# A two-layer hybrid decoder on one core: new order of the mixers' output projection and of the work around it, and seven low halves built by an adding transfer

## The chip, the cores and the metric

The kernel runs on one core of one Trainium2 chip. Its engines are TensorE (PE; its weight loads are listed as PEld), VectorE (DVE), ScalarE (ACT), GpSimd (POOL) and SyncE (SP), which issues nearly all transfers. The metric is the time of one execution on the device in microseconds, as the median of the runs.

## The reference

One sequence of 256 tokens with 1024 features passes through two layers. Each layer is FFN, mixer, FFN, and every part is wrapped in RMS norms:

```python
f = swiglu_ffn(rmsnorm(x, ffn1_norm_pre[i]), ffn1_w_in[i], ffn1_w_out[i])
x = x + 0.5 * rmsnorm(f, ffn1_norm_post[i])
h = rmsnorm(x, mix_norm_pre[i])
p = h @ mix_w_in[i]
qkv, z, beta_logit, a_logit, glu_in, gates = jnp.split(p, SPLITS, axis=-1)
y_a = gated_deltanet(qkv, z, beta_logit, a_logit, ...)
y_b = conformer_conv(glu_in, ...)
g_a, g_b = jnp.split(jax.nn.sigmoid(gates), 2, axis=-1)
y = (g_a * y_a + g_b * y_b) @ mix_w_out[i]
x = x + rmsnorm(y, mix_norm_post[i])
# and a second FFN as the first
```

`gated_deltanet` (8 heads of 128) runs a causal convolution of 4 taps and SiLU over q, k and v, normalizes q and k, solves a triangular system per chunk of 64 tokens, and scans over the chunks with a state per head; its output is normalized per head, `o = rmsnorm(o, norm_w) * silu(z)`, and multiplied by `gdn_w_o`. `conformer_conv` gates one half of its input by the sigmoid of the other, runs a causal convolution of 31 taps, a layer norm and SiLU, and multiplies by `cnv_w_o` and adds `b_o`. All is float32.

## The kernel before, in words

**Products in three parts.** Each float32 operand of a large product is split into a high half, rounded to the fast type, and a low half, the difference. A product is the sum of high by high, high by low and low by high, so each weight tile gives three PE instructions. The weights are cut into pieces of 128 x 1024 (512 KB). For every piece SP issues a transfer from memory to a tile `raw` (a ring of four), ACT rounds it to `whi` (`to_high`), and DVE or POOL subtracts: `wlo = raw - whi` (`to_low`); `whi` and `wlo` are rings of eight.

**The order of a mixer.** A mixer works off 17 chunks of columns of its input projection, in the order of the table `PLAN`: g0 to g3 (the convolution's input and its gates), k1, ka, kb (keys, and the logits of the decays), v, q, z, and a, b (the gates of the merger). Two further products with 1024 x 1024 weights follow, the heads' (`gdn_w_o`) and the convolution's (`cnv_w_o`), then the last with `mix_w_out`. In between run jobs of the other engines, each a generator that is moved on step by step: `f_*` takes a chunk's products out of the banks; `decays` and `dts` make the decays; `kt`, `qt`, `vt` the keys, queries and values (the short convolution's steps are `c`, its results `kT`, `qT`, `vT`); `sim` the similarities (`at`); `inv` the triangular inverse, on POOL (`iu`), whose result goes through memory (`dU`) into the tiles `u`; `merge` puts its blocks together on PE; `s0`, `s1` the scan (`vr`, `vn`, `o`); `c0` to `c3` the long convolution on DVE (`cacc`, `hT`); `cn`, `cn1` its norm (`bns`, `lnr`, `xhat`, transposed again and through SiLU into `cf` and `ct`); `on0`, `on` the norm of the heads (`vo`, `ro`, `ot`); `yt` the merged rows before the last product.

**What sets the order.** `PLAN` says at which chunk a job may start, `DELAY` how many groups of products lie between its steps, `AFTER` and `LATE` which jobs must be done before, and how long before. A planner counts time on the engines by simple costs (`vector_us`, `pool_us`) and gives each low half to DVE or POOL; DVE, POOL and ACT then work off their programs in exactly this order. `FILL` names the jobs that are used as filling, the long convolution on DVE and the inverse on POOL, in steps for which an engine has time (`ahead`, `aheadp`).

**The end of a mixer.** Before, the convolution's projection comes first: its eviction adds `b_o` and multiplies by the gate b. The heads' projection follows: its eviction multiplies by the gate a and adds the other. The normalization of q is not applied to q; the job `qs` computes `rq` and its square on POOL, and `o_scale` brings them into the norm of the heads.

Of the kernel before, what the change touches and what calls it, by code (L numbers as in the profile page):

```python
# [46 lines left out]
    "ffn": (3, 2, 8, 12, 0), "pre0": (12, 12, 10, 0, 21, 2), "pre1": (14, 43, 4, 12, 8), "yt0": (10, 0, 10, 10, 26),  # L47
    "yt1": (10, 2, 0, 3, 3), "f_g0": (3, 0, 2, 9, 1), "f_g1": (5, 1, 1, 1), "c0": (0, 16, 0),
    "f_k1": (0, 1, 3, 1, 1, 3), "f_ka": (3, 0, 3), "decays": (12, 4, 2, 15, 4), "dts": (50, 3, 0, 0, 19, 19),
# [15 lines left out]
    "qs": ("qt0", "qt1"), "s0": ("merge", "vt0", "vt1", "qt0", "qt1"), "s1": ("s0",),  # L65
    "cn": ("c0", "c1", "c2", "c3", "s1"), "cn1": ("cn",), "on": ("s1", "on0"), "on0": ("s0", "qs"),
# [6 lines left out]
LATE = {"inv": 20, "cn": 12, "sim0": 5, "sim1": 6, "merge": 7, "dts": 14}  # L73

POOL = {*range(7, 10), *range(11, 14), 16, *range(18, 21), 22, 23, 25, *range(29, 33), 35, 36, 38, 39, *range(41, 45), *range(47, 50), 51, 53, 55, 58, 60, 61, 63, *range(65, 69), *range(70, 73), 77, 78, 85}
# [11 lines left out]
CFG = dict(stat=1000, conv=50, ev=300, tok=4, st=4, post=-800, pre=1000, fin=None, turn=100, tokens=-100, glu=100, dec=200, dts=500, kt=300, vt=0, qt=50, inv=1000, sim=100, merge=-400, scan=50, norm=-800, onorm=-100, yt=-400, w=50, forms=100, far=14, depth=9, land=1.8, slack=1.2, apart=3, beat=1.0, tails=4, ahead=1.5, lag=6, free=3, aheadp=3, lag2=3, bias=2, held=1, urge=2.0, close=3.0)  # L87

KIND = {"f_g0": "glu", "f_g1": "glu", "f_g2": "glu", "f_g3": "glu", "decays": "dec", "dts": "dts", "kt0": "kt", "kt1": "kt",
        "vt0": "vt", "vt1": "vt", "qt0": "qt", "qt1": "qt", "qs": "qt", "inv": "inv", "sim0": "sim", "sim1": "sim",  # L90
# [237 lines left out]
class Stream:  # L328
# [51 lines left out]
    def load_one(self):  # L380
        i, p = self.nload, self.ringed()
        if self.planned:
            return
        c = slice(0, p.raw.src.shape[-1])
        if p.raw.tile is None:
            p.raw.tile = self.fresh()
            self.nc.sync.dma_start(p.raw.tile[:, c], p.raw.src)
        p.low = 0.0
        if self.lanes is not None:
            self.his.append((self.lanes.now + CFG["lag"], i, lambda: self.to_high(p, c)))  # L390
            self.lows.append((self.lanes.now + CFG["lag"] + CFG["lag2"], i, lambda eng: self.to_low(p, c, eng)))
# [12 lines left out]
    def tick(self, upto=-1):  # L404

        if self.planned:
            self.pump()
            return

        def due(job):  # L410
            return job[0] <= self.lanes.now or job[1] <= upto
        while self.his and due(self.his[0]):
            self.his.pop(0)[2]()
        while self.lows and due(self.lows[0]):
            job = self.lows.pop(0)
            first = self.gp.at + 2.4 <= self.vec.at + 1.2 + CFG["bias"] and job[1] < len(self.side) and self.gp.tc is not None
            job[2](self.gp if first else self.vec)

    def in_step(self, lanes):
        if lanes is None:  # L420
            self.tick(self.nload)
            self.lanes.stream = None
        else:
            lanes.stream = self
        self.lanes = lanes

    def plan(self, lanes):
        if lanes is not None:
            self.planned, self.lanes, lanes.stream, self.begun = True, lanes, self, self.pe.at
            self.raws = []  # L430
            for p in self.pieces[self.nload:self.nload + 120]:
                for raw in p.group:
                    if raw not in self.raws:
                        raw.first = p.n
                        self.raws.append(raw)
            self.out = []
        else:
            for p in self.pieces[self.taken:self.nload]:
                self.force(p)
            self.planned, self.lanes.stream, self.lanes = False, None, None  # L440

# [60 lines left out]
    def issue(self, eng, t, p, kind):  # L502
# [4 lines left out]
        for c in p.parts if p.form else [slice(0, n)]:  # L507
# [47 lines left out]
def trunk(ctx: ExitStack, tc: tile.TileContext, x_in, wfirst, consts, feat, pch, tokp,  # L555
# [103 lines left out]
    for l in range(depth):  # L659
# [10 lines left out]
        extend(m)  # L670
# [481 lines left out]
    def mixer(xt, l, after_mix):  # L1152
# [96 lines left out]
        rq = small(16, "rq", bufs=1)  # L1249
        rq2 = small(16, "rq2", bufs=1)  # L1250
# [257 lines left out]
        def q_tokens(gp):  # L1508
# [5 lines left out]
            V.tensor_scalar(vq[:, gp * 8:gp * 8 + 8], ss, float(P), P * 1e-6, op0=ALU.mult, op1=ALU.add)  # L1514
# [121 lines left out]
        def take(c):  # L1636
# [20 lines left out]
            "qs": lambda c: q_scale(), "cn": lambda c: conv_norm(), "cn1": lambda c: conv_out(1), "on": lambda c: o_norm(), "on0": lambda c: o_first(),  # L1657
# [76 lines left out]
        def o_scale(tb):  # L1734
# [5 lines left out]
            rqt, rq2t = (t.rearrange("p (g b h) -> p g b h", g=2, b=2)[:, :, tb, :] for t in (rq, rq2))  # L1740
# [36 lines left out]
        def ev_b(tb, acc):  # L1777
            for hf in range(2):
                cs = slice(hf * 512, hf * 512 + 512)
                yb = tokt("yb")  # L1780
                V.tensor_tensor(yb, acc[hf], bo[:, cs], op=ALU.add)
                gt = gate[f"b{hf}"][:, tb, :]
                V.scalar_tensor_tensor(gt, gt, 1.0, yb, op0=ALU.add, op1=ALU.mult)
# [3 lines left out]
        def ev_a(tb, acc):  # L1787
            yT[tb] = [slot(16 + 2 * hf + tb, [P, 2, 4, P], F32R, name="yt") for hf in range(2)]
            for hf in range(2):
                gt = gate[f"a{hf}"][:, tb, :]  # L1790
                V.scalar_tensor_tensor(gt, gt, 1.0, acc[hf], op0=ALU.add, op1=ALU.mult)
                V.tensor_tensor(gt, gt, gate[f"b{hf}"][:, tb, :], op=ALU.add)
# [134 lines left out]
```

## Time and profile before

| | |
|---|---|
| Runs | 1337.93, 1337.77, 1335.19 us |
| Median | 1337.77 us |
| The profiled execution, its own time | 1335.39 us |
| Its span, first to last instruction | 1333.2 us |
| Granted TensorE clock | 0.999 |
| PE busy | 1310.6 us, 98% of the span |
| DVE, ACT, POOL busy | 1031.1, 772.1, 369.4 us |
| Weights, one transfer from issue to landing (mixer) | 3.8 us |
| Moved in all | 273.78 MB |

The first layer's mixer lies at about 186 to 489 us of the span, the second's at about 847 to 1149. POOL works almost only in the mixers. The names to the left of an arrow are what an instruction writes, to the right what it reads; line numbers are often those of a helper through which all instructions of an engine pass (L134 for DVE and POOL, L154 and L160 for PE, L189 for ACT), so groups are told apart by names of tiles. Matmuls are pipelined, so PE's busy time counts an array that is fed without a break.

### The profile page before, as it was taken

The numbers are of one execution on the slowest core, as the hardware profiler recorded it, in microseconds if no ns is written. First come the engines' busy times: TensorE is split into PE (matmuls) and PEld (weight loads), VectorE is DVE, ScalarE is ACT, GpSimd is POOL, SyncE is SP. The second block draws the span as 40 slices with busy tenths as digits, with TensorE's granted clock in tenths as the row PEclk, the third lists the DMA queues.
The fourth block names the chain that finished last, engine by engine and source line by source line (L and its number), as shares of the span: only waits on it lengthen the run. The fifth ranks groups of instructions, "written<-read, shape, count | busy, mean of one in ns | idle before, by whom it ended". The sixth has DMA issues, their size and how long they took to land.

```text
span 1333.2 us, 20598 instructions
## 1 busy us (share of the span) xinstructions
PE 1310.6 (98%) x7376; PEld 1112.1 (83%) x7376; DVE 1031.1 (77%) x1812; ACT 772.1 (58%) x1263; POOL 369.4 (28%) x332
## 2 busy tenths in 40 slices
PE   9999999999999999999999999999999999999998
PEld 7887879997787888888888888799977878888886
DVE  6889655999975776897577895569999766678973
ACT  6566547676565545565455564577646664555751
POOL 0000017798853200000000000277998431000000
PEclk9999999999999999999999999999999999999999
DMA  8985846562643666858568768464536447587481
GB/s 300 305 268 157 297 158 206 175 209 100 191 149 137 229 231 211 263 176 275 189 234 271 239 193 273 138 234 165 186 119 200 157 135 246 176 279 243 155 295 50
DMA packets 115302, 273.78 MB, mean 205 GB/s; under 512 B 24160, under 2 KB 48256, under 8 KB 115200
## 3 DMA queue, kind: packets, MB, share of 16 engines
q1 hardware_dynamic: 114912, 272.40, 61.5%
q8 instruction: 58, 0.95, 0.3%
q14 instruction: 44, 0.36, 0.1%
q10 hardware_dynamic: 288, 0.07, 0.0%
HBM read 256.68 MB, written 15.75 MB: 204 GB/s over the span
## 4 chain that ended last, share of the span: by engine, by line
PE 74%; DVE 14%; ACT 4%; DMA 3%; issue 2%; POOL 1%; DVEq 0%; POOLq 0%; ACTq 0%; SPq 0%
PE mm L154 69%; DVE cacc L134 4%; DVE wlo L134 4%; PE gd L154 3%; DVE c L134 2%; DMA raw<-mw 2%; ACT whi L189 2%; PE tr L160 2%; DMA raw<-w1i 1%; DVE at L134 1%; ACT dt L189 1%; DVE sum L134 1%; ACT sg L189 0%; DMA raw<-w2i 0%; DVE qT L134 0%
## 5 line engine op out<-in xcount | busy, mean ns | idle before, releaser
L154 PE MATMUL mm<-whi,xt 128*128 128x512 f32 (+1 forms) x1888 | 598.7, 391 | 3.6 <-ACT qT L189 2.2
L189 ACT CAST whi<-raw 128x1024 fp32r<-128x1024 f32 (+1 forms) x424 | 435.0, 1035 | 282.7 <-PE mm L154 61.1
L134 DVE TENSOR_TENSOR wlo<-raw,whi 128x1024 fp32r<-128x1024 f32 (+1 forms) x316 | 377.0, 1211 | 110.3 <-ACT whi L189 107.6
L154 PEld LDWEIGHTS mm<-whi,xt 128*128 128x128 f32 x1888 | 352.5, 188 | 77.0 <-ACT qT L189 3.0
L154 PE MATMUL mm<-wlo,xt 128*128 128x512 f32 (+1 forms) x944 | 365.0, 387 | 0.0
L134 POOL TENSOR_TENSOR wlo<-raw,whi 128x1024 fp32r<-128x1024 f32 (+1 forms) x108 | 253.9, 2368 | 145.0 <-ACT whi L189 142.7
L154 PE MATMUL mm<-whi,act 128*128 128x512 f32 x704 | 218.5, 390 | 0.0
L154 PEld LDWEIGHTS mm<-wlo,xt 128*128 128x128 f32 x944 | 177.5, 188 | 34.0 <-DVE wlo L134 0.7
L134 POOL TENSOR_TENSOR rpost<-ss,exp 128x1 f32<-128x1 f32 x12 | 6.5, 539 | 661.8 <-DVE ss L134 661.8
L134 DVE SCALAR_TENSOR_TENSOR cacc<-hT,pc,cacc 128x254 f32<-128x254 f32 (+28 forms) x464 | 179.4, 467 | 0.2
L154 PE MATMUL mm<-xt,whi 128*128 128x256 f32 x960 | 175.5, 285 | 0.8 <-ACT qT L189 0.6
L154 PEld LDWEIGHTS mm<-whi,act 128*128 128x128 f32 x704 | 132.2, 188 | 27.8 <-DVE ag L134 0.5
L154 PEld LDWEIGHTS mm<-xt,whi 128*128 128x128 f32 x960 | 149.3, 192 | 1.9 <-ACT qT L189 0.9
L154 PE MATMUL mm<-wlo,act 128*128 128x512 f32 x352 | 137.2, 390 | 0.5 <-DVE wlo L134 0.5
L154 PE MATMUL mm<-xt,wlo 128*128 128x256 f32 x480 | 135.7, 283 | 0.0
L154 PEld LDWEIGHTS mm<-xt,wlo 128*128 128x128 f32 x480 | 91.9, 192 | 0.0
L154 PEld LDWEIGHTS mm<-wlo,act 128*128 128x128 f32 x352 | 66.1, 188 | 14.6 <-DVE wlo L134 1.2
L189 ACT ACTIVATE ag<-mm,rstd 128x256 f32<-128x256 f32 x80 | 35.4, 470 | 30.0 <-PE mm L154 28.5
L189 ACT ACTIVATE jk<-mm 128x512 f32<-128x512 f32 x24 | 14.4, 598 | 63.2 <-PE mm L154 63.2
L134 DVE TENSOR_TENSOR act<-way,act 128x512 fp32r<-128x512 f32 x44 | 30.3, 689 | 21.1 <-ACT act L189 21.1
L134 DVE SCALAR_TENSOR_TENSOR ag<-mm,rstd,ag 128x256 f32<-128x256 f32 x80 | 35.8, 479 | 13.5 <-ACT ag L189 13.5
L134 DVE SCALAR_TENSOR_TENSOR c<-mm,pc,c 128x255 f32<-128x255 f32 (+2 forms) x108 | 43.7, 476 | 2.3 <-ACT c L189 2.3
(217 smaller groups left out, 1457.6 us busy)
## 6 DMA issues: line engine op xcount, KB each, us to landing
raw<-mw SPq DMA_DIRECT2D x168, 512.0 KB, 3.8
raw<-w2i SPq DMA_DIRECT2D x80, 512.0 KB, 4.9
raw<-w1i SPq DMA_DIRECT2D x76, 512.0 KB, 4.9
raw<-w1o SPq DMA_DIRECT2D x44, 512.0 KB, 4.5
raw<-w2o SPq DMA_DIRECT2D x44, 512.0 KB, 4.7
way<-way SPq DMA_DIRECT2D x112, 64.0 KB, 2.3
way<-way SPq DMA_DIRECT2D x28, 256.0 KB, 4.0
wbc<-feat SPq DMA_DIRECT2D x13, 512.0 KB, 5.0
```

Source lines behind the costliest of these rows:

```text
L134: r = op(out, *a, **k)
L154: r = self.eng.matmul(o, w, x, **k)
L160: r = self.eng.transpose(*a)
L189: r = op(out, *a, **k)
```

## The change

Six things change, in both mixers alike; the order of the chunks and PE's number of products stay.

1. The heads' projection comes first, the convolution's second, with the pieces of their weights in that order too. The heads' eviction (`ev_o`) multiplies by gate a and adds gate b times `b_o`; the convolution's (`ev_c`) multiplies by gate b and adds. One more DVE operation for each half row.
2. The job `qs` is gone. The sum of q's squares is scaled with the norm's epsilon, and `o_scale` forms its denominator with one DVE operation where POOL had two, and no product by `rq` after the power.
3. `PLAN`, `DELAY` and `LATE` are new, which moves jobs against the chunks.
4. The planner's cost of a DVE operation, its lead on POOL and its bias between DVE and POOL are a little different.
5. `ADDS` names pieces by their number within a mixer, seven of which exist. For these ACT writes the negative of the high half into the low half's tile (a second instruction of 1024 columns), and POOL issues a transfer that fetches the weights from memory again and adds them there. No `raw - whi` is computed for them.
6. Where the tables of ACT's functions change, its program has 14 table loads in all, before 10.

Counted over the program: POOL's tensor operations 302 to 274 (16 of the 28 are low halves), its small scalar operations 8 to 4, its transfers 0 to 14; DVE 978 three-operand steps where 966 were and two more low halves; ACT 14 more activations.

```diff
+ADDS = set((3, 9, 27, 31, 32, 34, 47, 51, 54, 55, 58, 59, 61))
...
+            self.fed += 1
+            p.adds = self.fed in ADDS
...
             self.act.copy(p.hi[:, c], p.raw.part(c))
+            if p.adds:
+                self.act.activation(p.lo[:, c], p.hi.bitcast(F32)[:, c], AF.Copy, scale=-1.0)
+
+    def add_raw(self, p):
+        with prio(self.tc, "w"):
+            self.gp.dma_start(p.lo[:, :p.raw.src.shape[-1]], p.raw.src, accum_op=ALU.add)
...
             job = self.lows.pop(0)
+            if job[3].adds:
+                self.add_raw(job[3])
+                continue
...
-        extend(m)
+        m = list(m)
+        extend(m[8:16] + m[:8] + m[16:])
...
-            V.tensor_scalar(vq[:, gp * 8:gp * 8 + 8], ss, float(P), P * 1e-6, op0=ALU.mult, op1=ALU.add)
+            V.tensor_scalar(vq[:, gp * 8:gp * 8 + 8], ss, P * RMS_EPS, P * 1e-6 * RMS_EPS, op0=ALU.mult, op1=ALU.add)
...
-        def q_scale():
-            yield from ()
-            power(rq, vq, -0.5)
-            W.tensor_tensor(rq2, rq, rq, op=ALU.mult)
...
-            W.tensor_tensor(ve, rq2t, sso, op=ALU.mult)
-            W.tensor_scalar(v8, v8, 1.0 / P, RMS_EPS, op0=ALU.mult, op1=ALU.add)
+            V.scalar_tensor_tensor(ve, sso, 1.0 / P, vqt, op0=ALU.mult, op1=ALU.add)
             power(r8, v8, -0.5)
-            W.tensor_tensor(ro, ro, rqt, op=ALU.mult)
...
+        lanes.finish(last["on"])
+        proj_out(head_part, 8, ev_o)
         lanes.finish(last["cn"])
-        proj_out(lambda kt, tb: part(cT[tb], kt), 8, ev_b, need=lambda: last["cn1"])
-        lanes.flush()
-        proj_out(head_part, 8, ev_a)
+        proj_out(lambda kt, tb: part(cT[tb], kt), 8, ev_c, need=lambda: last["cn1"])
```

How the order moves is shown at three places of the first mixer. The first is PE around the convolution's norm: `hT` is the convolution's output, `xhat` its normalized rows, `ct` what the convolution's projection multiplies and `ot` what the heads' does. Before:

```order
L154 MATMUL mm<-wlo,xt 128x512
L154 MATMUL mm<-whi,xt 128x512
L160 MATMUL tr<-cst,hT_1787 128x128 x4
L160 MATMUL tr<-cst,hT_1788 128x128 x4
L160 MATMUL tr<-cst,xhat 128x128 x8
L154 MATMUL mm<-whi,ct 128x512
L154 MATMUL mm<-wlo,ct 128x512
```

and now:

```order
L179 MATMUL tr<-cst,hT_1787 128x128 x4
L179 MATMUL tr<-cst,hT_1788 128x128 x4
L173 MATMUL mm<-whi,ot 128x512
L173 MATMUL mm<-wlo,ot 128x512
L173 MATMUL mm<-whi,ot 128x512 x2
L173 MATMUL mm<-wlo,ot 128x512
L173 MATMUL mm<-whi,ot 128x512
L179 MATMUL tr<-cst,xhat 128x128 x4
L173 MATMUL mm<-whi,ot 128x512
```

The transposes of `xhat` stood right behind those of `hT` and right ahead of the products that read their result; they now stand among the products of the heads' projection, and four at a time.

The second is ACT at the decays, whose exponentials are `aexp` and `eo`; `kT` is the keys' SiLU and `sg` the sigmoid of the convolution's gates, read from the banks that PE fills next. Before:

```order
L189 ACT_TABLE_LOAD
L189 ACTIVATE aexp<-tp 128x16
L189 ACTIVATE eo<-ba 128x16
L189 CAST whi<-raw 128x1024
L189 ACTIVATE eo<-ein 128x16
L189 CAST whi<-raw 128x1024
L189 ACTIVATE sg<-mm,bgh 128x256
L189 ACTIVATE sg<-sg 128x256
L189 CAST whi<-raw 128x1024
L189 ACTIVATE sg<-mm,bgh 128x256
```

and now:

```order
L208 ACTIVATE eo<-ba 128x16
L208 CAST whi<-raw 128x1024
L208 ACT_TABLE_LOAD
L208 ACTIVATE kT_1790<-c_2136 128x256
L208 ACT_TABLE_LOAD
L208 ACTIVATE eo<-ein 128x16
L208 ACTIVATE sg<-mm,bgh 128x256
L208 CAST whi<-raw 128x1024
L208 ACTIVATE sg<-sg 128x256
L208 CAST whi<-raw 128x1024
L208 ACT_TABLE_LOAD
L208 ACTIVATE kT_1790<-c_2137 128x256
```

Two steps of `kT`, which stood ahead of this stretch, now lie within it, each behind a table load of its own, and another load leads back to the exponential.

The third is POOL at the end of the inverse (`iu`) in the first mixer. Before:

```order
L134 TENSOR_TENSOR iu<-iu 128x14x4
L134 TENSOR_TENSOR wlo<-raw,whi 128x1024
L134 TENSOR_TENSOR iu<-iu,ia 128x45
L134 TENSOR_TENSOR iu<-iu 128x15x3
L134 TENSOR_TENSOR iu<-iu,ia 128x30
L134 TENSOR_TENSOR iu<-iu 128x15x2
L134 TENSOR_TENSOR iu<-iu,ia 128x16
L134 TENSOR_TENSOR iu<-iu 128x16
L134 TENSOR_TENSOR wlo<-raw,whi 128x1024 x5
L134 TENSOR_TENSOR rq<-vq,exp_80 128x16
```

and now:

```order
L153 TENSOR_TENSOR iu<-iu,ia 128x70
L153 TENSOR_TENSOR iu<-iu 128x14x5
L153 DMA wlo<-mw 128x1024
L153 TENSOR_TENSOR iu<-iu,ia 128x56
L153 TENSOR_TENSOR iu<-iu 128x14x4
L153 TENSOR_TENSOR iu<-iu,ia 128x45
L153 TENSOR_TENSOR iu<-iu 128x15x3
```

The row `DMA wlo<-mw` is an adding transfer that POOL issues; four of them stand between steps of the inverse, and one low half that POOL computes. Before, two low halves stood there.

More of the change, by code (lines that the diff above doesn't have):

```diff
@@ L38 @@
 PLAN = [
[4 rows of a table removed]
+    ("g0", ["f"]),
+    ("k1", ["f", "sim1", "c1"]),
+    ("ka", ["f", "decays", "dts"]),
+    ("g1", ["f", "c0", "inv", "kt1"]),
+    ("kb", ["f", "kt0"]),
+    ("g3", ["f", "sim0"]),
+    ("g2", ["f"]),
+    ("v1", ["f", "vt1", "c3"]),
+    ("q0", ["f", "s1", "qt1", "c2", "vt0"]),
+    ("q1", ["f", "s0"]),
+    ("v0", ["f", "qt0"]),
+    ("z0", []),
+    ("z1", ["merge", "on0", "on"]),
+    ("a0", []),
+    ("b0", ["cn1"]),
+    ("b1", []),
+    ("a1", ["cn"]),
 ]
@@ L46 @@
     "first": (0,), "forms": (57, 0, 6, 0, 1), "begun": (1, 0), "later": (0, 0, 1, 1), "gate": (0, 1), "gates": (0, 1, 1),
[L47 to L49 removed]
[8 rows of a table removed]
+    "ffn": (3, 2, 8, 12, 0), "pre0": (10, 12, 18, 0, 21, 1), "pre1": (15, 35, 4, 4, 0), "yt0": (7, 1, 0, 27, 3),
+    "yt1": (2, 12, 0, 11, 4), "f_g0": (0, 8, 0, 3, 21), "f_g1": (0, 5, 2, 3), "c0": (24, 16, 11),
+    "f_k1": (4, 2, 13, 1, 0, 3), "f_ka": (4, 0, 8), "decays": (12, 4, 3, 15, 4), "dts": (0, 3, 0, 0, 32, 8),
[8 rows of a table added]
 }
@@ L64 @@
     "qt0": ("f_q0", "vt0"), "qt1": ("f_q1", "vt1"),
-    "qs": ("qt0", "qt1"), "s0": ("merge", "vt0", "vt1", "qt0", "qt1"), "s1": ("s0",),
-    "cn": ("c0", "c1", "c2", "c3", "s1"), "cn1": ("cn",), "on": ("s1", "on0"), "on0": ("s0", "qs"),
+    "s0": ("merge", "vt0", "vt1", "qt0", "qt1"), "s1": ("s0",),
+    "cn": ("c0", "c1", "c2", "c3", "s1"), "cn1": ("cn",), "on": ("s1", "on0"), "on0": ("s0", "qt0", "qt1"),
 }
@@ L71 @@
 FILL = (("c3", "c2", "c1", "c0"), ("inv",))
-LATE = {"inv": 20, "cn": 12, "sim0": 5, "sim1": 6, "merge": 7, "dts": 14}
-POOL = {*range(7, 10), *range(11, 14), 16, *range(18, 21), 22, 23, 25, *range(29, 33), 35, 36, 38, 39, *range(41, 45), *range(47, 50), 51, 53, 55, 58, 60, 61, 63, *range(65, 69), *range(70, 73), 77, 78, 85}
+LATE = {"inv": 23, "cn": 7, "sim0": 3, "sim1": 5, "merge": 0, "dts": 14, "qt1": 0, "kt0": 1, "vt1": 14, "s0": 3, "qt0": 0, "vt0": 20, "s1": 0, "kt1": 0}
+POOL = {9, 10, 12, 13, 22, 23, 25, 26, 27, 30, 31, 32, 35, 38, 41, 42, 44, 46, 47, 53, 54, 56, 58, 59, 63, 64, 65, 66, 67, 70, 72, 73, 78, 82, 85}
 UNITS = 4*((9,),)
@@ L85 @@
 USERS = {"12": (("t1", "summed"),), "22": (("22", "low"), ("t2", "summed")), "11": (("t3", "low"),), "21": (("21", "low"), ("t4", "summed"))}
-CFG = dict(stat=1000, conv=50, ev=300, tok=4, st=4, post=-800, pre=1000, fin=None, turn=100, tokens=-100, glu=100, dec=200, dts=500, kt=300, vt=0, qt=50, inv=1000, sim=100, merge=-400, scan=50, norm=-800, onorm=-100, yt=-400, w=50, forms=100, far=14, depth=9, land=1.8, slack=1.2, apart=3, beat=1.0, tails=4, ahead=1.5, lag=6, free=3, aheadp=3, lag2=3, bias=2, held=1, urge=2.0, close=3.0)
+ADDS = set((3, 9, 27, 31, 32, 34, 47, 51, 54, 55, 58, 59, 61))
+CFG = dict(stat=1000, conv=50, ev=300, tok=4, st=4, post=-800, pre=1000, fin=None, turn=100, tokens=-100, glu=100, dec=200, dts=500, kt=300, vt=0, qt=50, inv=1000, sim=100, merge=-400, scan=50, norm=-800, onorm=-100, yt=-400, w=50, forms=100, far=14, depth=9, land=1.8, slack=1.2, apart=3, beat=1.0, tails=4, ahead=1.5, lag=6, free=3, aheadp=3.5, lag2=3, bias=1.5, held=1, urge=2.0, close=3.0)
 KIND = {"f_g0": "glu", "f_g1": "glu", "f_g2": "glu", "f_g3": "glu", "decays": "dec", "dts": "dts", "kt0": "kt", "kt1": "kt",
-        "vt0": "vt", "vt1": "vt", "qt0": "qt", "qt1": "qt", "qs": "qt", "inv": "inv", "sim0": "sim", "sim1": "sim",
+        "vt0": "vt", "vt1": "vt", "qt0": "qt", "qt1": "qt", "inv": "inv", "sim0": "sim", "sim1": "sim",
         "merge": "merge", "s0": "scan", "s1": "scan", "cn": "norm", "cn1": "norm", "on": "onorm", "on0": "onorm",
@@ L104, in pool_us, with plain_us @@
     return 0.2 + (4e-3 if name == "tensor_scalar" else 1e-3) * size
+def plain_us(name, size, k):
+    return 0.1 + size / 960.00
 class Clocked:
@@ L301, in __init__ @@
         self.raw, self.form, self.use, self.n = raw, form, use, 0
+        self.adds = False
         self.hi = self.lo = self.summed = self.high = self.low = None
@@ L389, in load_one @@
         if self.lanes is not None:
+            self.fed += 1
+            p.adds = self.fed in ADDS
             self.his.append((self.lanes.now + CFG["lag"], i, lambda: self.to_high(p, c)))
-            self.lows.append((self.lanes.now + CFG["lag"] + CFG["lag2"], i, lambda eng: self.to_low(p, c, eng)))
+            self.lows.append((self.lanes.now + CFG["lag"] + CFG["lag2"], i, lambda eng: self.to_low(p, c, eng), p))
             return
@@ L423, in in_step @@
         else:
-            lanes.stream = self
+            lanes.stream, self.fed = self, 0
         self.lanes = lanes
@@ L515, in issue @@
                 self.to_low(p, c, eng)
+        if eng is self.vec:
+            k = len(p.parts if p.form else [0])
+            eng.at = t + k * 0.1 + n / 960.0
         setattr(p, {"sum": "summed"}.get(kind, kind), eng.at)
@@ L1774, in mixer, with ev_o @@
         bo = load_feat(l, R_BO, 4)
[L1777 to L1783, printed above, removed]
-        yT = [None, None]
-        def ev_a(tb, acc):
-            yT[tb] = [slot(16 + 2 * hf + tb, [P, 2, 4, P], F32R, name="yt") for hf in range(2)]
+        def ev_o(tb, acc):
             for hf in range(2):
@@ L1791, in ev_a, with ev_c @@
                 V.scalar_tensor_tensor(gt, gt, 1.0, acc[hf], op0=ALU.add, op1=ALU.mult)
-                V.tensor_tensor(gt, gt, gate[f"b{hf}"][:, tb, :], op=ALU.add)
+            for hf in range(2):
+                gt, yb = gate[f"a{hf}"][:, tb, :], tokt("yb")
+                V.scalar_tensor_tensor(yb, gate[f"b{hf}"][:, tb, :], 1.0, bo[:, hf * 512:hf * 512 + 512], op0=ALU.add, op1=ALU.mult)
+                V.tensor_tensor(gt, gt, yb, op=ALU.add)
+        yT = [None, None]
+        def ev_c(tb, acc):
+            yT[tb] = [slot(16 + 2 * hf + tb, [P, 2, 4, P], F32R, name="yt") for hf in range(2)]
+            for hf in range(2):
+                gt, gb = gate[f"a{hf}"][:, tb, :], gate[f"b{hf}"][:, tb, :]
+                V.scalar_tensor_tensor(gb, gb, 1.0, acc[hf], op0=ALU.add, op1=ALU.mult)
+                V.tensor_tensor(gt, gt, gb, op=ALU.add)
             def steps():
```

10 lines of the change are left out of this document (5 added, 5 removed), and 20 rows, old and new, of tables (DELAY, PLAN).

## The prediction

> **What bounds the kernel now.** I read the page first, then the busy time by stage, then what the tensor engine waits for in each mixer, then the chain around its longest waits. The page's share of busy time and its chain:
>
> ```profile
> PE 1310.6 (98%) x7376; PEld 1112.1 (83%) x7376; DVE 1031.1 (77%) x1812; ACT 772.1 (58%) x1263; POOL 369.4 (28%) x332
> PE 74%; DVE 14%; ACT 4%; DMA 3%; issue 2%; POOL 1%; DVEq 0%; POOLq 0%; ACTq 0%; SPq 0%
> ```
>
> PE leaves 1333.2 - 1310.6 = 22.6 us free in the whole span. The windows say where (first layer: four pieces of the mixer, then the FFN ahead of it and the two behind it; columns: us, busy time of each engine with its instructions, granted clock, DMA share, GB/s):
>
> ```profile
> 176.00:254.00 78.00, 76.33 (x507) 69.17 (x506) 54.86 (x124) 51.65 (x89) 41.98 (x23) 1.00 0.56 184
> 254.00:330.00 76.00, 72.82 (x559) 69.42 (x557) 75.07 (x185) 49.21 (x94) 69.38 (x88) 1.00 0.52 170
> 330.00:389.00 59.00, 57.80 (x584) 47.35 (x585) 51.42 (x131) 37.05 (x77) 40.40 (x28) 1.00 0.53 165
> 389.00:500.00 111.00, 108.89 (x545) 90.88 (x544) 78.58 (x114) 58.00 (x109) 30.15 (x22) 1.00 0.56 193
> 1.00:176.00 175.00, 174.18 (x765) 141.21 (x766) 132.68 (x191) 103.28 (x152) 1.09 (x2) 1.00 0.78 258
> 500.00:835.00 335.00, 335.00 (x1487) 276.69 (x1486) 255.73 (x345) 187.37 (x255) 2.70 (x5) 1.00 0.70 231
> ```
>
> The FFNs are full. The mixer leaves 1.67 + 3.18 + 1.20 + 2.11 = 8.16 us free, and from 254 to 330 DVE is as full as PE (75.07 of 76). A change inside the mixers that keeps PE's products can win those 8 us a layer and no more. PE's waits, the first mixer (176 to 500) and then the second (835 to 1160):
>
> ```profile
> PE tr L160 <- ACT cf L189: 1.7, 1, 1.7
> PE tr L160 <- ACT vT L189: 1.5, 1, 1.5
> PE mm L154 <- ACT qT L189: 1.4, 2, 1.1
> PE gd L154 <- ACT sq L189: 1.0, 1, 1.0
> PE tr L160 <- ACT stg L189: 0.9, 1, 0.9
> ```
> ```profile
> PE tr L160 <- ACT cf L189: 1.7, 1, 1.7
> PE tr L160 <- ACT vT L189: 1.5, 1, 1.5
> PE mm L154 <- ACT qT L189: 1.4, 2, 1.1
> PE tr L160 <- ACT stg L189: 0.7, 1, 0.7
> ```
>
> These are 6.5 and 5.3 us. The queue that loads PE's weights was held a little longer by the same five (first mixer):
>
> ```profile
> PEld mm L154 <- ACT qT L189: 2.0, 2, 1.5
> PEld tr L160 <- ACT cf L189: 2.0, 1, 2.0
> PEld tr L160 <- ACT vT L189: 2.0, 2, 1.7
> PEld gd L154 <- ACT sq L189: 1.4, 1, 1.4
> PEld tr L160 <- ACT stg L189: 1.1, 1, 1.1
> ```
>
> That is 8.5; in the same proportion the second mixer has 5.3 x 8.5/6.5 = 6.9. So 11.8 us of waiting by the first count, 15.4 by the second.
>
> **The change part by part.** PE's 6874 products and transposes stay, and so does the order of the chunks: PE gains only what it doesn't wait.
>
> *Convolution's norm (cf).* Before, the first eight transposes of the normalized convolution stand side by side ahead of the convolution's projection, which needs them at once; PE waits 1.7. Now they stand four at a time between products of the heads' projection, and what comes of them is needed a whole projection later. Gain 1.7 a layer (2.0 by the weight queue).
>
> *Short convolutions (qT, vT).* PE waits there for ACT, and ACT for DVE, which runs in one list. In program order between v1's first products and the first of z0, that list loses ten of 54 steps of the long convolution (cacc), two of 48 short steps (c), two of six low halves and six `at`. Their rates stand in the chain:
>
> ```profile
> 313.81 2.34 DVE c L134 x6
> 339.94 5.10 DVE cacc L134 x14
> 317.70 1.13 DVE wlo L134
> ```
>
> 10 x 0.364 + 2 x 0.39 + 2 x 1.13 = 6.7 us, and `at` besides. The longest of these waits is 1.7, so they go: 2.9 a layer. The steps come back before the scan's `vr` of the second block, where DVE had idled until PE delivered:
>
> ```profile
> 389.12 0.35 DVE L134 SCALAR_TENSOR_TENSOR vr<-gd,neg_eg,vr 128x128 f32<-128x128 f32 x1 [7.42 <-PE gd L154]
> ```
>
> 6.7 of 7.42 us is just covered; with PE 4 us earlier by then, it could be short by 3. I take 0.5, bounds 0 and 3.
>
> *Merge (sq).* The chain around that wait:
>
> ```profile
> 345.05 3.84 DMA raw<-mw
> 348.97 1.05 ACT whi L189
> 350.01 0.51 ACT sq L189
> 350.56 0.45 PE gd L154 x24
> ```
>
> `sq` stands on ACT behind a high half whose weights SP issued only after the eight transfers of the inverse. In the new order `sq` stands behind halves whose weights are issued ahead of those transfers. Gain 1.0 in the first mixer.
>
> *Staging (stg).* Fewer high halves stand ahead of the copy that the transposes need: 0.9 and 0.7.
>
> *Two more table loads.* ACT's program now has `kT` of the first half between the two Exp of the decays, so four table loads stand where two stood. Before:
>
> ```profile
> 226.70 1.04 ACT L189 CAST whi<-raw 128x1024 fp32r<-128x1024 f32 x1
> 227.76 1.28 ACT L189 ACT_TABLE_LOAD   x1
> 229.05 0.22 ACT L189 ACTIVATE aexp<-tp 128x16 f32<-128x16 f32 x1
> 232.55 0.42 ACT L189 ACTIVATE sg<-sg 128x256 f32<-128x256 f32 x1
> 237.19 0.40 PE L154 MATMUL mm<-xt,whi 128*128 128x256 f32 x2
> ```
>
> ACT comes to the first load at 227.74. From there to the read that frees g3's bank, the new order has four loads (4 x 1.28 = 5.1), three high halves (3 x 1.04 = 3.1), three small Exp (0.11 apart, 0.3), two `kT` and three `sg` (about 0.35 apart, 1.8): 227.74 + 10.3 = 238.0. PE wants that bank where it stood at 237.2: 0.8 late, and some 0.2 of handing over. I take 1.0 a layer, with bounds 0 (ACT starts earlier, as PE does) and 2.3 (it doesn't, and PE comes 1 us sooner).
>
> The row shows the next instruction 0.01 us after the load's end. The Trainium skill (ScalarE: Activation LUTs, "What ACT_TABLE_LOAD costs") gives 1283 ns for the load, as here, but adds a drain of 1380 ns to each switch; by that rule the two extra loads would hold ACT 2.8 us longer a layer and the gain would be some 5.5 us smaller in all. No drain shows in the rows around this load.
>
> *Seven low halves by adding transfers, per layer.* Each replaces a subtraction (POOL 2.37, DVE 1.13) by a second copy on ACT (the shape of `whi`, 1.04) and a transfer that POOL issues, which fetches the weights again. ACT gains 7.3 us a layer, at 58% busy. The traffic is 14 x 0.52 = 7.3 MB on 273.78, the DMA share in the mixer is 0.52 to 0.56: room. Four of the issues stand inside the inverse, which POOL works off in order; what is behind them is the rest of the inverse, and for that wait its transfers and the merge. POOL's rows (first mixer, the two products of the inverse and the low halves; then its result's transfers on SP):
>
> ```profile
> L134 POOL TENSOR_TENSOR wlo<-raw,whi 128x1024 fp32r<-128x1024 f32 x12 | 30.1, 2526 | 2.8 <-ACT whi L189 2.7
> 336.05 0.23 POOL L134 TENSOR_TENSOR iu<-iu 128x16 f32<-128x16 f32 x1
> L1422 SPq DMA_DIRECT2D dU<-iu x2: 604/1129/1654, 336.3 to 337.0; - x2
> L1427 SPq DMA_DIRECT2D u<-dU x8: 303/446/521, 340.7 to 344.6; - x8
> DMA to landing us min/median/max: 1.7/3.1/4.1
> 349.19 0.39 PE L154 MATMUL mm<-whi,xt 128*128 128x512 f32 x1
> ```
>
> The inverse ended at 336.28. Now one low half less stands ahead of it and one less inside: 2 x 2.4 = 4.8 earlier, 331.5 + 4c, where c is POOL's time for one issue, waiting for ACT's copy included. From its end to the last of `u` landed it took to about 344.6 + 2.4 = 347.0, so 10.7. PE is ready for the merge at 349.6, less the 3.8 of waits removed ahead of it, plus 1.0 lost: 346.8. So c up to (346.8 - 331.5 - 10.7)/4 = 1.2 us costs nothing, and beyond it each mixer loses 4(c - 1.2). No POOL issue is in this trace. Nearest below: SP's shortest issue of `u`, 0.3; above: one pass of POOL over such a tile, 2.4. I take 1.1, as the median issue of `dU<-iu`: no loss; at 2.4 it is 4.8 a layer.
>
> *Heads first, q's scale folded in.* POOL loses two small operations and three of four around each `ro`, DVE gets one more there and four in the evictions. What was hidden behind the convolution's projection, the norm of `o`, now has only the end of chunk a1. Its parts are short:
>
> ```profile
> 390.95 1.64 POOL L134 TENSOR_TENSOR ro<-vo,exp 128x8 f32<-128x8 f32 x1
> ```
>
> With eight squares on ACT (0.5 with their reads, about 4.5 in all with `gate` between), this 1.64 and eight scalings on DVE at 0.27 (2.2), it needs about 8.4; PE has 46 products ahead of the transposes, 9.9 us at their pitch. Covered by 1.5; if not, 0 to 2 lost. With the rest of a new order I allow 0.5 a layer.
>
> **The sum.** Waits removed 11.8 to 15.4; I take 13.0, nearer PE's own count. Lost per layer 1.0 + 0.5 + 0 + 0.5 = 2.0, so 4.0. Net 9.0. The profiled execution took 1335.39 and becomes 1326.4. It lies 2.4 below the median of the runs (1337.77) and 0.2 above their fastest; I put the forecast between, at **1327.5** us.
>
> **The rivals.** 0.2% is 2.7 us, about what a measurement here can tell from nothing: faster is below 1335.1, slower above 1340.5.
>
> - *No new wait* (0.15): 15.4 gained and nothing lost, 1320. For it: the bounds 0 of each loss. Against it: ACT's list at the decays is longer by two loads whatever PE does.
> - *The waits move* (0.17): `vr` short by 3, ACT's read by 2.3, `o` by 1: 6.3 a layer, 12.6 against 11.8 to 13: 1335 to 1336, no change. For it: DVE's total hardly falls, and 254 to 330 was full. Against it: three upper bounds at once.
> - *POOL's issue is dear* (0.16, slower): with c above 1.2 + (9.0 + 2.7)/8 = 2.7 us the inverse comes so late that both mixers lose more than they won. At c = 3.5 it is 8 x 2.3 - 9.0 = 9.4 more: 1345. For it: 69.38 of 76 us POOL was busy there, nothing can be made up, and the issue also stands behind ACT's copy. Against it: no row near it costs over 2.4.
> - *The change does nothing* (0.02): DVE, not its order, sets the pace; then the waits for qT and vT stay.
>
> What would make c large: the Trainium skill (SBUF — State Buffer, "Who interferes with whom") says that descriptors of a transfer issued by GpSimd wait while VectorE runs a copy or tensor_scalar in a two-port mode, and measured 3.1 us for what takes 0.62 alone. With that c, 7.6 a layer would be lost and the time be 1342. In this mixer nearly all DVE rows are two-input operations, to which that page gives no such mode, so I hold it to a part of the 0.16.
>
> **Chances.** Forecast 0.50 (own range 1322 to 1333), the rivals as given. Faster: 0.50 + 0.15 + 0.08 of the moved waits = 0.73; same: the other 0.09 and 0.02 = 0.11; slower 0.16. The range, 1318 to 1341, leaves out the dear issue and the tail of a clean win.
>
> **What would show it.** Right: the rows for cf, qT, vT and sq are gone from PE's waits in both mixers, a wait of about 1 us for `sg` is there, POOL's inverse ends before 334 and the merge waits for nothing. Wrong: PE waits for `u` or for a low half that came by an adding transfer, or for `vr` or `ot` by 2 us or more; or the FFNs or the clock differ.

## The result and the profile after

The changed kernel takes 1324.53 us (median of 5; 1323.58 to 1326.12) against 1337.77 (median of 5; 1335.19 to 1339.79): a ratio of 0.9905, with a 95% interval of 0.9889 to 0.9921. That is 13.2 us less; 10.3 less were predicted, and the range of 1318 to 1341 holds it. The profiled execution took 1323.58 with a span of 1321.8, 11.4 less than the span before.

The page of the changed kernel, busy time and chain:

```profile
PE 1308.9 (99%) x7376; PEld 1111.4 (84%) x7376; DVE 1036.6 (78%) x1826; ACT 789.5 (60%) x1281; POOL 334.3 (25%) x314
PE 76%; DVE 11%; DMA 5%; ACT 3%; issue 2%; POOL 2%; SPq 0%; DVEq 0%; POOLq 0%; ACTq 0%
```

PE is free for 12.9 us where it was for 22.6, which is 9.7 of the 11.4; the other 1.7 lies in its modelled busy time, with the same number of instructions. The windows of the first mixer, as in the prediction:

```profile
176.00:254.00 78.00, 77.74 (x520) 70.73 (x519) 54.34 (x116) 56.64 (x94) 35.27 (x21) 1.00 0.64 200
254.00:330.00 76.00, 74.57 (x573) 71.59 (x572) 71.39 (x180) 54.94 (x104) 68.64 (x92) 1.00 0.66 202
330.00:389.00 59.00, 59.00 (x585) 48.27 (x585) 58.40 (x145) 37.29 (x78) 38.70 (x26) 1.00 0.68 193
389.00:500.00 111.00, 110.81 (x551) 92.23 (x550) 81.81 (x128) 60.39 (x106) 22.33 (x15) 1.00 0.52 180
```

The first mixer's 8.16 us of PE's free time are 0.26 + 1.43 + 0 + 0.19 = 1.88. In the second mixer (835 to 1160) PE was free for 6.54 us before and is for 1.86 now. DVE's work has moved as the order said: 75.07 became 71.39 in the second window and 51.42 became 58.40 in the third, where PE is full all the same. PE's waits in the first mixer (176 to 500; the second shows the same four and one of 0.2 for `xw`):

```profile
PE mm L173 <- DVE hT L153: 0.9, 1, 0.9
PE tr L179 <- ACT vr L208: 0.4, 1, 0.4
PE mm L173 <- DVE c L153: 0.2, 1, 0.2
PE mm L173 <- DVE ss L153: 0.2, 1, 0.2
```

cf, qT, vT, sq and stg are gone wherever they stood. One wait is new, 0.9 for `hT`. POOL in the first mixer's inverse (its first and last step, and the first and last of the four issues between them), and the group of all its transfers:

```profile
295.20 0.24 POOL L153 TENSOR_TENSOR iu<-iu,ia 128x31 f32<-128x31 f32 x1 [0.93 <-DMA ia<-dA]
300.89 0.95 POOL L153 DMA_DIRECT2D wlo<-mw  x1
...
329.03 0.88 POOL L153 DMA_DIRECT2D wlo<-mw  x1 [0.15 <-issue]
332.82 0.24 POOL L153 TENSOR_TENSOR iu<-iu 128x16 f32<-128x16 f32 x1
wlo<-mw POOLq DMA_DIRECT2D x14, 512.0 KB, 7.3
```

An issue in the inverse takes POOL 0.88 to 0.95 us, and its transfer lands 7.3 us later in the median (the mixer's weights that SP issues: 4.3, before 3.8). The inverse ends at 333.06.

### The profile page after: what moved, and what is told of

Read it like the earlier page. It is cut to its first block, busy times and chain, and to the rows that moved or that the text cites. A ratio compares the mean times of both kernels' runs of the same rounds, so it can differ in the third digit from the quotient of the medians.

```text
span 1321.8 us, 20648 instructions
## 1 busy us (share of the span) xinstructions
PE 1308.9 (99%) x7376; PEld 1111.4 (84%) x7376; DVE 1036.6 (78%) x1826; ACT 789.5 (60%) x1281; POOL 334.3 (25%) x314
## 4 chain that ended last, share of the span: by engine, by line
PE 76%; DVE 11%; DMA 5%; ACT 3%; issue 2%; POOL 2%; SPq 0%; DVEq 0%; POOLq 0%; ACTq 0%
PE mm L173 70%; DVE wlo L153 5%; PE gd L173 4%; DMA raw<-w1i 3%; PE tr L179 2%; DVE cacc L153 2%; ACT whi L208 1%; DMA way<-way 1%; DVE sum L153 1%; DMA raw<-w2i 1%; DVE c L153 1%; DVE ag L153 1%; POOL rk L153 1%; DVE way L153 0%; ACT dt L208 0%
## 5 line engine op out<-in xcount | busy, mean ns | idle before, releaser
L153 DVE TENSOR_TENSOR wlo<-raw,whi 128x1024 fp32r<-128x1024 f32 (+2 forms) x318 | 384.8, 1230 | 120.3 <-ACT whi L208 118.8
L153 POOL TENSOR_TENSOR wlo<-raw,whi 128x1024 fp32r<-128x1024 f32 (+1 forms) x92 | 216.4, 2365 | 131.0 <-ACT whi L208 116.8
```

The costliest lines, as they stand in the source:

```text
L153: r = op(out, *a, **k)
```

## The experiments

All ratios are against the kernel before, timed beside each run.

**Without the adding transfers.**

```diff
-ADDS = set((3, 9, 27, 31, 32, 34, 47, 51, 54, 55, 58, 59, 61))
+ADDS = set()
```

> The changed kernel without its adding transfers: the planner gives the seven low halves per mixer back to POOL (102 in all where the change has 92) and DVE (322 for 318). Theory A (the order of jobs and of the projections carries the gain; the transfers only take work from POOL, which is off PE's path): the inverse starts about 3 us later (two more low halves at 2.4 ahead of it for two issues at 0.9) and has 4.8 us of low halves inside where the change has 2.4 + 4 x 0.9 = 6.0, so it ends about 1.8 us later; from the last transfer of u to the merge the change shows 1 to 2 us of cushion, so 0 to 1 us a mixer is lost: 1324 to 1327 us. Theory B (the transfers carry a good part of the gain by freeing POOL and DVE): waits for u, vT or qT come back and the time is 1330 us or more.

1367.93 us, 1.0235 (1.022 to 1.025): 43 us slower than with them, three times the whole gain. Theory A is out by 41 us. The time and the waits for `vT` are as theory B has them, its reason (POOL's and DVE's time) is not: the inverse is not late, it ends at 334.4, 1.4 us later than with them. PE waits in the first mixer, SP's waits from 290 to 345, and the chain there:

```profile
PE tr L179 <- ACT vT L208: 15.5, 3, 8.8
```
```profile
SPq L407 <- POOL wlo L153: 25.0, 4, 15.5
SPq L1457 <- POOL iu L153: 9.2, 1, 9.2
```
```profile
322.12 2.35 POOL wlo L153
...
324.49 3.49 DMA raw<-mw
...
328.05 1.04 ACT whi L208
329.10 0.38 ACT c L208
...
335.89 3.96 DMA raw<-mw
...
340.89 0.42 ACT vT L208
```

Two blocks follow each other. First, SP cannot issue the next weights (L407) because the tile they go to is still to be read by a low half that stands on POOL behind steps of the inverse; ACT, which works in order, stands 10.5 us at a high half with `c` and `vT` behind it. Then the weights after those stand on SP behind the transfer of the inverse's result (L1457), which waits for POOL; ACT stands 7.9 us more. So it is not in the first place POOL's time that the transfers buy. The next experiments on them (low halves on DVE, SP's order, POOL at the same places) take the two blocks apart.

**The old order of the projections, all else new.**

```diff
+        lanes.finish(last["cn"])
+        proj_out(lambda kt, tb: part(cT[tb], kt), 8, ev_b, need=lambda: last["cn1"])
+        lanes.flush()
+        proj_out(head_part, 8, ev_a)
-        lanes.finish(last["on"])
-        proj_out(head_part, 8, ev_o)
-        lanes.finish(last["cn"])
-        proj_out(lambda kt, tb: part(cT[tb], kt), 8, ev_c, need=lambda: last["cn1"])
```

(the evictions and the order of the weights are those of before, too)

> The changed kernel, with the convolution's projection first and the heads' second as before, and the evictions of before; tables, adding transfers and the folded scale of q stay. Theory A (the new tables place the convolution's norm so late that only the heads' projection covers it): the whole chain of the norm, about 10 us of transposes, statistics, power, SiLU and low halves, stands open ahead of the convolution's projection, 5 to 10 us a mixer: 1334 to 1345 us. Theory C (each of the two projections has its norm ready anyway, and the order only takes away the wait for cf): 1.7 to 2.0 us a mixer come back: 1328 to 1329 us.

1341.62, 1.0034 (1.002 to 1.0048). Theory A: what it loses against the changed kernel lies at the convolution's norm, which has no cover.

```profile
PE tr L179 <- DVE xhat L153: 5.6, 2, 4.0
```

PE stands 4.1 and 1.9 us beyond its usual pitch in the first mixer, 4.1 and 2.3 in the second, 12.4 in all; the span is 16.3 longer. The rest goes with the clock, which falls in the windows behind the wait (the last columns: granted clock, DMA share, GB/s):

```profile
412.00:416.00 4.00, 0.67 (x5) 0.49 (x6) 2.24 (x6) 0.00 (x0) 2.25 (x2) 0.99 0.54 202
416.00:418.00 2.00, 1.05 (x4) 0.64 (x4) 1.26 (x4) 0.86 (x3) 0.55 (x1) 0.50 0.19 76
418.00:420.00 2.00, 1.34 (x6) 1.27 (x7) 1.90 (x4) 1.46 (x5) 0.00 (x0) 0.50 0.00 0
420.00:422.00 2.00, 2.00 (x6) 1.62 (x5) 0.38 (x2) 1.89 (x6) 0.00 (x0) 0.50 0.00 0
422.00:424.00 2.00, 2.00 (x8) 1.59 (x8) 0.38 (x2) 0.00 (x0) 0.00 (x0) 0.81 0.00 0
```

**The kernel before with the new order of the projections alone** (the two calls, evictions and weights of the experiment above, the other way round).

> The kernel before with one part of the change alone: the heads' projection first, the convolution's second, with the new evictions. Theory A (order and tables work only together): the wait for cf goes, 1.7 to 2.0 us a mixer, but the norm of the heads, which the tables of before start at the end of the chunks, stands open for up to its 8 us chain: between 1334 and 1350 us, slower than before more likely than not, with waits for ot or o in place of cf. Theory C (the order alone earns cf's wait): 1333 to 1335 us.

1357.99, 1.016 (1.014 to 1.0179), slower than expected at worst. The wait for cf is gone, and in its place:

```profile
PE mm L154 <- DVE ct L134: 2.3, 1, 2.3
PE mm L154 <- ACT ct L189: 2.0, 1, 2.0
PE tr L160 <- DVE ot L134: 1.8, 1, 1.8
PE tr L160 <- DVE xhat L134: 1.6, 1, 1.6
```

Both norms stand open, since the old tables have neither ready, and the granted clock falls again, to 0.78 and 0.50 between 450 and 458. The order of the projections is worth having only with the tables that go with it.

**The kernel before with the adding transfers alone** (the `ADDS` branch of the diff for the same seven pieces).

> The kernel before with the adding transfers alone, for the same seven pieces of each mixer. Theory A: PE's waits for cf, stg and sq stay as they are; DVE has two low halves less a mixer (2.3 us), so the waits for qT and vT may shrink by up to that; four issues of 0.9 us in the inverse replace two low halves of 2.4, so it ends a little earlier: 1333 to 1338 us. Theory B (freed POOL and DVE carry the gain): the waits for qT and vT are gone and the time is under 1331 us.

1337.98, 1.0002 (0.9991 to 1.0013): nothing, as theory A had it. The waits for cf and qT stay, vT's shrinks by 0.5:

```profile
PE tr L162 <- ACT cf L191: 1.7, 1, 1.7
PE mm L156 <- ACT qT L191: 1.4, 2, 1.1
PE tr L162 <- ACT vT L191: 1.0, 1, 1.0
```

So with the old tables the low halves in the inverse hold nobody up for long, and only with the new ones are they to be gone; that this comes of q's and v's work, which the new tables move against the inverse, is argued and not shown. In the old tables `sq` is free of its wait, which is made up by more of `vr` (1.6 in place of 0.4).

**The seven low halves on DVE.**

```diff
-                self.add_raw(job[3])
+                job[2](self.vec)
                 continue
```

(ACT's negative copies fall away, too)

> The changed kernel, where the seven low halves of each mixer that came by an adding transfer are subtracted by DVE at the same place in the program; ACT's negative copies fall away. Without the transfers (first experiment) ACT stood 10.5 and 7.9 us for weights whose transfer SP could not issue, since the tile it goes to (a ring of four) was still to be read by a low half queued on POOL inside the inverse. Theory D (what the adding transfer buys is that its tile comes free as soon as ACT has read it, not POOL's time): DVE also frees the tile in time, the long waits for vT stay away, and only DVE's own 4 x 1.13 us in the full stretch count, against 4.6 us that DVE has free there: 1325 to 1334 us. Rival E (DVE is too full to take them): waits for vT and qT of several us a mixer, 1336 us or more.

1388.23, 1.0374 (1.035 to 1.0398). Rival E's size, but not its reason: DVE was less busy than ever there (60.07 of 76 us). ACT stood 27.4 us for one weight tile. SP's order in this kernel has four weight transfers between the inverse's input and `dU`, and then (waits of SP, 290 to 345, and its program):

```profile
SPq L1455 <- POOL iu L153: 27.9, 1, 27.9
```
```profile
293.45 10.81 SPq L407 DMA_DIRECT2D raw<-mw  x4
332.26 1.31 SPq L1455 DMA_DIRECT2D dU<-iu  x2
333.67 1.13 SPq L407 DMA_DIRECT2D raw<-mw  x2
```

`dU` reached the head of SP's queue 27.9 us before the inverse was done, and all weights stood behind it. The number of weight transfers ahead of `dU` in the program is 11 in the changed kernel, 11 before, 8 without the adding transfers and 4 here.

**Adding transfers in the inverse only.**

```diff
+ADDS = set((27, 31, 32, 34))
```

> The changed kernel with adding transfers for four of the seven pieces only, those whose issue stands inside the inverse; the other three go where the planner puts them. Theory D: these four carry all that the transfers give, 1323 to 1328 us. Rival F (it is POOL's time over the whole mixer that counts, or the pieces ahead of the inverse): half of the loss of the first experiment or more comes back, 1345 us or more.

1324.80, 0.9907 (0.9886 to 0.9928): as the changed kernel. The other three transfers of each mixer do nothing for the time.

**The inverse made longer.**

```diff
+                if s % 4 == 2:
+                    at = W.at
+                    W.memset(buf[:, 0:512], 0.0)
+                    W.at = at
```

> The changed kernel with eight more POOL fills of 128 x 512 (0.52 us each) spread over the inverse, 4.1 us a mixer, which the planner does not see; they write a scratch tile. In the changed kernel the last transfer of u is issued at 341.1 and lands 1.9 to 3.5 us later, the merge starts at 345.3: 0.7 to 2.3 us of cushion. If the inverse is as close to the path as the prediction put it (cushion 4 x 1.2 less 4 x 0.9 = 1.2 us): 1.8 to 3.4 us a mixer lost, 1328 to 1332 us, with waits for u. If the inverse is off the path: 1324 to 1326 us.

1330.12, 0.995 (0.9934 to 0.9967): 5.6 us more than the changed kernel, 2.8 a mixer for 4.1 of fill, so POOL's program has a cushion of about 1.3 us a mixer; the runs lie between 1327.97 and 1334.03, so this is known to about 1 us. The waits that came are not for `u` by name:

```profile
PE gd L173 <- ACT at L208: 1.1, 1, 1.1
PE mm L173 <- DMA wlo<-mw: 0.9, 1, 0.9
PE gd L173 <- ACT sq L208: 0.6, 1, 0.6
```

A part is the merge, held by the eviction between its groups. By the chain that eviction (`at`, 351.06) stands on ACT behind a high half (350.01) whose weights SP issued only after the last transfer of `u` (346.70). A part, 0.9 us here and 1.4 in the second mixer, is an adding transfer, issued later, that PE now waits for. The inverse itself became 5.2 us longer (295.44 to 338.45), more than the fill, so 1.3 is not the cushion of the inverse alone.

**g2's gate earlier.**

```diff
-    ... "f_g2": (0, 4, 3, 6), ...
+    ... "f_g2": (0, 4, 3, 0), ...
```

> The changed kernel with one delay altered, that of the last step of g2's job (6 to 0), so that the DVE step hT that frees g2's last bank stands ahead of a group of similarities and not behind it. The changed kernel waits there 0.9 us a mixer by PE's row (1.05 against its usual pitch). Theory: that wait goes, 1.8 to 2.1 us in all: 1322 to 1323.5 us. Rival: the similarities, 0.5 us later, pass it on to the inverse, whose cushion is 0.7 to 2.3: no change, 1324 to 1325 us.

1330.17, 0.9948 (0.9927 to 0.9969): slower than the changed kernel by 5.6. The wait for `hT` is gone, and a larger one has come, neither where the theory nor where the rival looked. DVE, then PE:

```profile
275.98 0.48 DVE L153 SCALAR_TENSOR_TENSOR hT<-mm,pc,sg 128x256 f32<-128x256 f32 x1 [1.63 <-ACT sg L208]
```
```profile
PE mm L173 <- DVE c L153: 3.3, 1, 3.3
```

`hT` now stands at the head of DVE's queue before ACT has its gate; DVE loses 1.63 us, and with the steps that now stand ahead of `c` v1's bank comes free 3.3 us late. The granted clock from 254 to 330 is 0.98, where the changed kernel has 1.00.

**The low halves on DVE, with SP's order mended.** As the experiment with DVE, with the planner's clocks as for the transfers, and:

```diff
-                nc.sync.dma_start(dv[par], ur[par * 64:par * 64 + 64])
+                r = nc.sync.dma_start(dv[par], ur[par * 64:par * 64 + 64])
+                behind(tc, getattr(r, "ins", r), st.fetched)
```

> As the experiment with the seven low halves on DVE (1388 us, where ACT stood 27 us for weights), but the planner's clocks are charged as for the adding transfers, and the transfer of the inverse's result (dU) is tied behind the last weights fetched ahead of it in the program, so that on SP ten weight transfers stand between the inverse's input and dU, where that experiment had four, and the changed kernel has eleven. Theory G (SP works off its queue in order; dU waits there for the inverse on POOL, and all weights behind it with it): the waits for vT of 16 to 20 us a mixer go, and DVE's four low halves in the full stretch cost at most 4.5 us a mixer: 1325 to 1334 us. Rival (DVE is too full for them, or what PE lacks are the low halves themselves): 1350 us or more.

1345.36, 1.0055 (1.0033 to 1.0077), between the two forecasts: 43 us less than the kernel that has DVE's low halves and the wrong order on SP. The wait for vT, 19.3 us in the first mixer, is gone altogether, which is theory G's point, and SP stands 12.0 us for the inverse with `dU` where it stood 27.9. The clocks and SP's order were changed together, so the 43 us are not split between them. What is left is more than it allowed, and of DVE's making:

```profile
PE mm L173 <- DVE hT L153: 3.1, 1, 3.1
PE tr L179 <- DVE o L153: 2.8, 1, 2.8
```

So DVE is too full for the seven in this order of jobs, at some 10 us a mixer with what the clock adds (0.98 in two of the four windows).

**POOL subtracts where it issued.** The same clocks, `job[2](self.gp)` in place of the transfer; ten weight transfers ahead of `dU`.

> The changed kernel, where POOL subtracts the seven low halves at the places in its program where it issued the adding transfers, with the planner's clocks charged as for these; ten weight transfers stand ahead of dU on SP (eleven in the changed kernel). Only POOL's time: 4 x (2.4 - 0.9) = 6 us more inside the inverse; by the experiment with the longer inverse (4.1 us more cost 2.8 a mixer) that is about 4.5 us a mixer: 1332 to 1335 us. Theory D (a low half queued on POOL between steps of the inverse holds one of the four weight tiles, so that SP's next transfer, ACT's next high half and vT behind it stand still): waits of ACT for raw and of PE for vT of 5 us or more a mixer on top, 1342 us or more.

1342.40, 1.0036 (1.0022 to 1.005): theory D. With ten weight transfers ahead of `dU`, the first block stands alone, in the chain of the first mixer:

```profile
320.87 2.37 POOL wlo L153
323.25 3.48 DMA raw<-mw
326.82 1.04 ACT whi L208
327.86 0.38 ACT c L208
```

ACT stood 7.6 us for these weights, and PE 6.2 for vT. A low half on POOL's queue holds its weight tile as long as the inverse steps ahead of it last; the adding transfer reads the weights from memory again, and lets the tile go when ACT has read it. The inverse is longer here as well, 296.62 to 339.60, or 43.0 us where the changed kernel has 37.9. PE shows no wait for that, since it comes to the merge late by the waits for vT; but the experiment that lengthened the inverse as much lost 5.6 us, so not all of the 18 us need be the tile's.

**g2's gate a little earlier** (`"f_g2": (0, 4, 3, 3)`).

> The changed kernel with the last delay of g2's job 3 where it was 6 (0 in the experiment before, which lost 5.6 us because DVE then stood 1.6 us for ACT's gate and so freed v1's bank late). Now DVE's step hT stands behind the second group of similarities, ahead of four steps that begin the next convolution (1.4 us). Theory: the wait of 0.9 us a mixer for hT goes, and DVE stands at most 0.4 us for the gate: 1322 to 1324 us. Rival: DVE's standing is passed on to v1's bank as before: 1325 to 1330 us.

1325.98, 0.992 (0.9901 to 0.994): the rival, at the lower end, and by the time not to be told from the changed kernel. `hT` is gone from PE's waits, and 1.5 us for `c` (v1's bank) are there instead: the same wait, one bank later.

**Two table loads less.**

```diff
-    ... "f_ka": (4, 0, 8), ...
+    ... "f_ka": (4, 0, 14), ...
```

> The changed kernel with the last delay of ka's job 14 where it was 8: the two steps kT move behind both Exp of the decays and ACT has 10 table loads in all, as before, where the change has 14. All other engines keep their programs. In the changed kernel ACT came to its first load 1.6 us earlier than before and no wait for sg shows. Theory (the loads lie in ACT's slack): no change, 1323.5 to 1326 us. Rival (the loads cost PE the 1.0 us a mixer that the prediction put there, hidden in other waits): 1322 to 1323 us.

1324.20, 0.990 (0.9882 to 0.9918): no change against 1324.53. The loads lie in ACT's slack. No version of these beat the changed kernel by more than a measurement can tell.

## Why the prediction was right, and where not

*The cap and the five waits.* That the gain lies in PE's waits inside the mixers, and can be no more than their 8 us, held. The first mixer won 6.28 us by the windows where the five rows promised 6.5, the second 4.68 where four rows promised 5.3. All these rows are gone. That is 10.96 us, of the 11.4 by which the span is shorter (over the whole span PE's free time fell by only 9.7, because the windows of the FFNs, 1 to 176 and 500 to 835, have 1.2 us more of it than before); the profiled executions differ by 11.8 us and the medians by 13.2, so 1.4 us of the 13.2 lie between executions, not in these traces.

*The sum of the waits.* I took 13.0 for both mixers. The rows of the five make 11.8, and two waits I had left standing shrank as well: in the first mixer those for `xt` and `ss`, 0.6 and 0.4, are together 0.2 now. So 13.0 was near, though not for its reason (the weight queue's longer count).

*The losses.* I put 2.0 us a layer, and a layer shows 0.9. This is the mis-sized term; 2.2 us for both layers, of the 3 between 1327.5 and 1324.5.

- Table loads: 1.0 a layer predicted, none measured, and the wait of about 1 us for `sg` that was to show it is not there. The list was right, its start was not: I began it at 227.74, where ACT stood before. Ahead of that lay two steps of `kT` with their waits for DVE, the same two that the list counts a second time inside. Before, with these, and now (load, first exponential, and the read that frees the bank):

```profile
225.71 0.42 ACT L189 ACTIVATE kT<-c 128x256 f32<-128x256 f32 x1 [0.62 <-DVE c L134]
226.38 0.42 ACT L189 ACTIVATE kT<-c 128x256 f32<-128x256 f32 x1 [0.25 <-DVE pre_a L134]
226.12 1.28 ACT L208 ACT_TABLE_LOAD   x1
227.42 0.22 ACT L208 ACTIVATE aexp<-tp 128x16 f32<-128x16 f32 x1
236.13 0.46 ACT L208 ACTIVATE sg<-mm,bgh 128x256 f32<-128x256 f32 x1
```

  Without the two, the last high half ahead of the load ends at 226.11 where it ended at 227.74, so ACT comes to the list 1.6 us sooner. The list was put at 10.3 us and is 10.5 long (226.12 to 236.59), and PE's first product into that bank starts at 236.70. The bound of 0 ("ACT starts earlier, as PE does") was the case, but by 0.1 us: with the old order of the projections and the same tables PE waits 0.4 us for this read. The experiment with ten loads shows that in the changed kernel they cost nothing. No drain shows: the next instruction starts 0.02 us after the load's end. The Trainium skill (ScalarE: Activation LUTs, "What ACT_TABLE_LOAD costs") adds a drain of 1380 ns to each switch; this trace does not agree.
- `vr`: 0.5 allowed, bounds 0 and 3; nothing came.
- The new order: 0.5 allowed; `hT` takes 0.9. Two tries to remove it only moved it.

*The inverse.* c was put at 1.1; a row of an issue is 0.88 to 0.95 long, and the next step starts 0.60 to 0.70 us after the issue's start. The prediction's end, 331.5 + 4c, is 335.9 with its own c, which its sign "before 334" did not allow, and 335.1 with 0.9. It is 333.06. The first step starts 2.5 us earlier (295.20 for 297.74), about as taken (2.4); but the two low halves inside had taken 5.8 and not 4.8, so that one of 2.4 in their place saves 3.4, and the four issues put the next steps off by only 2.5: 336.28 - 2.5 - 3.4 + 2.5 = 332.9. The merge waited for nothing, as said. With c = 0.9 the prediction's cushion is 4 x (1.2 - 0.9) = 1.2, beside about 1.3 by the longer inverse; both are rough, and that they agree proves little. That an issue of over about 1.2 us would have cost was not run. By the Trainium skill (SBUF — State Buffer, "Who interferes with whom") a transfer issued by GpSimd can stand because VectorE keeps GpSimd from writing its descriptors. The issues show no sign of it: four of 0.9 beside a DVE that is busy 71 of 76 us. Whether a part of the 7.3 us to landing is such a wait, no run shows.

*Heads first.* The norm of `o` is covered, as worked out; it is so by the new tables alone, as the kernel before with the new order shows.

*What the adding transfers are for.* Here the reasoning was wrong, and that the sum did not feel it was luck. The step "each replaces a subtraction (POOL 2.37, DVE 1.13)" took them for a saving of POOL's and DVE's time, with the danger on POOL's queue. The runs show that four of seven matter, that POOL's time is not what is lost without them (the inverse ends at 334.4 and, with them, at 333.06), and that they free two queues: the weight tile that a low half on POOL holds (experiment with POOL at the same places: at most 18 us), and the place of `dU` among the weights on SP, which the program's scheduler sets (the pair of runs with DVE: 43 us, together with the planner's clocks). Alone, on the kernel before, they give nothing. Why the scheduler puts `dU` so early without them is open.

*Two slips without effect.* The prediction's 6874 products and transposes are 7376 instructions on both pages. Its 46 products ahead of the transposes of `o` take 10.4 us at the 0.227 between two of them in the trace before, not 9.9.

## What to carry to other kernels

Where tiles go round in a small ring, ask for each reader of a tile which queue it stands in: a reader behind a long chain on an idle-looking engine stops the loads, and through an in-order engine work that has nothing to do with it. A transfer that waits for a slow chain should stand on its queue behind every load that is needed before that chain ends; count the loads ahead of it in the program. Parts of a change whose order was fitted together are not worth testing as a sum of parts: here the two parts tried alone gave nothing or lost 20 us, and all together gave 13.

## What the hardware showed that was not expected

A PE wait of some 2.5 us or more costs more than its length: the kernel with the old order of the projections lost 16.3 us to 12.4 us of waits. Behind the wait of 4.1 us at the convolution's norm the granted clock is 0.50 for six us and 0.81 in the next two, quoted above. A single wait of 2.5 us in the kernel without adding transfers was enough (PE's row, and the windows with the wait and behind it):

```profile
PE tr L179 <- DVE o L153: 2.5, 1, 2.5
420.00:424.00 4.00, 1.46 (x8) 0.97 (x7) 4.00 (x6) 0.32 (x1) 3.59 (x2) 1.00 0.42 131
424.00:428.00 4.00, 4.00 (x14) 3.23 (x14) 3.46 (x8) 1.73 (x2) 0.00 (x0) 0.65 0.41 131
```

From 426 to 428 it is 0.50. The 3.3 us in the kernel with g2's gate earlier are followed by 0.53 and 0.62 in windows of 2 us, and two waits of 2.0 and 2.3 us with two products between them did it in the kernel before with heads first. A single wait of 2.0 us (`hT`, low halves on DVE) did not, nor did the 1.7 us in the kernel before: 1.00 in the windows around. The Trainium skill (TensorE: Matmul & The Clock Gate, "What's actually happening") has it that the clock is halved after an idle window of about 3.4 us; here 2.5 us of waiting were enough. It does not enter the comparison of the two kernels, whose clock is 0.999 in both, but it widens the loss of every experiment that made PE wait for long.
